# A two-layer hybrid decoder trunk: a fixed order for the opening, modulation handed out beside the first mixer's products, and linear attention in other memory

## The chip, the core and the metric

The kernel runs on one core of a Trainium2 chip. Its engines are TensorE (PE, with weight loads as PEld), VectorE (DVE), ScalarE (ACT), GpSimd (POOL) and SyncE (SP), which issues most DMAs. The metric is the device time of one execution in microseconds (us), as the median of several runs.

## What is computed

The reference is a trunk of two layers over 1024 positions of width 1024, in float32. Cut to what matters:

```python
cond = silu(c)
for l in range(2):
    sh1, sc1, gt1, sh2, sc2, gt2 = split(cond @ w_mod[l] + b_mod[l], 6)
    h = rms_norm(x, norm_g[l, 0]) * (1 + sc1) + sh1
    z = split_cols(h @ w_in[l])                  # one projection for four groups of width 256
    outs = [short_conv(z), nsa(z), gla(z), gmlp(z)]
    y = concat(rms_norm(o, grp_gain) for o in outs) @ w_o[l]
    x = x + gt1 * rms_norm(y, norm_g[l, 1])
    h = rms_norm(x, norm_g[l, 2]) * (1 + sc2) + sh2
    y = square(relu(h @ w_up[l])) @ w_down[l]    # 1024 -> 4096 -> 1024
    x = x + gt2 * rms_norm(y, norm_g[l, 3])
```

`short_conv` is a gated convolution of width 3; `nsa` is attention over compressed, selected and window keys, with rotated queries and keys; `gla` is gated linear attention in chunks; `gmlp` mixes 128 positions at a time with a triangular matrix.

## The kernel before

**Tiling.** The sequence is cut into two halves of T = 512 positions, kept transposed: a tile is 128 channels by 512 positions, and x is eight such tiles. Layer l and half hf make one `mix(l, hf)` and one `ff(l, hf)`. Products are made in float32 accuracy from rounded parts: each operand is split into a high and a low part, and `mm3` (lines 172 to 175) does three matmuls for each 128 rows of the sum. A `gemm` has eight such steps, 24 matmuls of 512 columns; its weight comes in two halves of 256 KB, each split by `wunit`, the high part by a cast on ACT (L167) and the low part by a subtraction on DVE (L131).

**Lanes.** A weight goes through the buffers of a lane: "a" and "b" with three raw buffers and four for the parts, "f" for the feed-forward part with more. Lane "b" exists during the first mixer alone; its region is released for the feed-forward lane afterwards.

**Order.** The program is written as straight code; a scheduler in the compiler orders the instructions of all engines by its own timeline, with priorities. `high_priority(offset=-LATER[l, hf])` puts the residual and the norm at the end of a mixer later (lines 950 to 956). Once compiled, each engine runs its instructions in one fixed order.

**Opening.** `start()` (L265) makes cond, loads x for half 0, makes the first norm's R (ones-product L195, ACT L199 and L200), the first two modulation vectors by dots on DVE (L239, one for every 128 outputs, two for every k) and, for each k of eight, h (L207 to L210) and one step of `mm3` for the six outputs in EARLY, so that 18 matmuls follow on each h. Their weights are w_k, in two sets of six. `rope_tables` (L339) makes cosines and sines on DVE, transposes them (L375), multiplies by a selection (L380), copies (L377, L382) and writes both to DRAM.

**First mixer.** `mix(0, 0)` runs its attention (`nsa_part`: probabilities bp are transposed into ps_t, L777, split into w_a at L779 and L131, and multiplied by values, L782 and L783) beside linear attention (`gla_part`: for each j of four a score product L592, copies, a select on POOL L596, products L602 and L605). Then come `gmlp_part` and `conv_part`, whose regions take the memory of linear attention, and then `mods_now(0, (2, 3, 4), "b")`: 48 dots on DVE (L247), each on a load of 256 KB, for the modulation that is needed behind w_o. w_o's eight gemms (L943) end in a copy to yo (L946). `norm(0, 1, xt)` of the other half stands behind them.

**End of ff(1, 0).** In the last group of `down` eight sums are added into the tiles yf (L137) of region "fin", which lies where region "wo" of `mix(1, 1)` lay. The residual (L226) and `make_h` (L203) of `mix(1, 1)` go on at that time.

## Time and profile before

| what | value |
|---|---|
| median of 3 runs | 2635.78 us (2635.64 to 2638.55) |
| profiled execution | 2634.88 us, span 2633.1 us, mean granted clock 0.975 |
| PE busy | 2488.4 us, 95% of the span |
| DVE, ACT, POOL busy | 1631.0, 1310.5, 53.0 us |
| DMA | 305.79 MB, mean 116 GB/s |

A stretch in which PE is busy for less than its length, or at a granted clock under 1, is where time can be had; who released PE at the end of an idle time is given behind the arrow in the rows.

### The profile page before, as it was taken

To read this page: it belongs to the slowest core of one execution; us is meant where nothing else is said; L and a number is where in the kernel's file an instruction comes from. 1 tells how busy PE (TensorE), PEld (TensorE's weight loads), DVE (VectorE), ACT (ScalarE), POOL (GpSimd) and SP (SyncE) were. 2 spreads that over 40 slices of the span, in tenths; PEclk is the share of its full clock that TensorE was granted. 3 is DMA by queue.
4 is the path that set the end of the run, shared out by engine and by line. 5 is a ranking of instruction groups with operands and counts; after the bars stand their busy time and mean duration, and the time that the engine had idled before them with its cause. 6 is when DMAs were issued, how large, how long until landed. Compare 5 with 4: busy or idle time off the path is not lost.

```text
span 2633.1 us, 34406 instructions
## 1 busy us (share of the span) xinstructions
PE 2488.4 (95%) x11834; PEld 1987.3 (75%) x11834; DVE 1631.0 (62%) x3425; ACT 1310.5 (50%) x2657; POOL 53.0 (2%) x65
## 2 busy tenths in 40 slices
PE   5899499999999999999999999999999998899997
PEld 3666277777877878887787878877788876788886
DVE  7676866557888577444676476544567755634445
ACT  3573345445665356344366445444466744443333
POOL 0100000000000000000100000000100000000000
PEclk9899699999999999999999999999999999999999
DMA  8313634345434454322522344322322134433332
GB/s 279 100 46 100 203 117 132 106 140 153 129 123 134 155 164 140 102 85 89 154 83 70 116 152 140 99 84 79 119 77 68 57 108 143 136 97 96 97 97 75
DMA packets 176200, 305.79 MB, mean 116 GB/s; under 512 B 21573, under 2 KB 33434, under 8 KB 176026
## 3 DMA queue, kind: packets, MB, share of 16 engines
q1 hardware_dynamic: 176026, 303.60, 36.7%
q8 instruction: 93, 1.52, 0.2%
q14 instruction: 81, 0.66, 0.1%
HBM read 281.50 MB, written 17.83 MB: 114 GB/s over the span
## 4 chain that ended last, share of the span: by engine, by line
PE 83%; DVE 6%; DMA 4%; issue 1%; ACT 1%; POOL 0%; DVEq 0%; SPq 0%; ACTq 0%; POOLq 0%
PE ps_ff L173 16%; PE ps_ff L174 16%; PE ps_ff L175 16%; PE ps_mm L173 8%; PE ps_mm L175 8%; PE ps_mm L174 8%; DMA raw_f<-in_w_mod_dram 2%; PE ps_pv L783 1%; PE ps_mm L777 1%; PE ps_pv L782 1%; PE ps_s L822 1%; DMA raw_b<-in_w_mod_dram 1%; PE ps_s L824 1%; PE ps_t L777 1%; PE ps_t L195 1%
## 5 line engine op out<-in xcount | busy, mean ns | idle before, releaser
L167 ACT CAST w_f<-raw_f 128x512 fp32r<-128x512 f32 x504 | 311.7, 619 | 426.3 <-PE ps_ff L174 409.2
L131 DVE TENSOR_TENSOR w_f<-raw_f,w_f 128x512 fp32r<-128x512 f32 x504 | 350.4, 696 | 178.7 <-ACT w_f L167 167.9
L173 PE MATMUL ps_ff<-hid,w_f 128*128 128x512 f32 x992 | 395.4, 399 | 21.7 <-DVE yf L137 12.7
L175 PE MATMUL ps_ff<-h,w_f 128*128 128x512 f32 x1024 | 405.4, 396 | 1.2 <-DVE w_f L131 1.2
L173 PE MATMUL ps_ff<-h,w_f 128*128 128x512 f32 x1024 | 403.1, 394 | 0.0
L174 PE MATMUL ps_ff<-h,w_f 128*128 128x512 f32 x1024 | 402.3, 393 | 0.0
L174 PE MATMUL ps_ff<-hid,w_f 128*128 128x512 f32 x992 | 392.4, 396 | 1.5 <-DVE hid L131 1.5
L175 PE MATMUL ps_ff<-hid,w_f 128*128 128x512 f32 x992 | 391.7, 395 | 0.0
L173 PE MATMUL ps_mm<-h,w_a 128*128 128x512 f32 x784 | 318.2, 406 | 32.6 <-ACT yo L946 23.7
L175 PE MATMUL ps_mm<-h,w_a 128*128 128x512 f32 x784 | 317.2, 405 | 6.0 <-DVE w_a L131 6.0
L174 PE MATMUL ps_mm<-h,w_a 128*128 128x512 f32 x784 | 314.8, 403 | 3.6 <-DVE h L131 3.6
L167 ACT CAST w_a<-raw_a 128x512 fp32r<-128x512 f32 x196 | 121.3, 620 | 304.5 <-PE ps_mm L174 278.7
L131 DVE TENSOR_TENSOR w_a<-raw_a,w_a 128x512 fp32r<-128x512 f32 x196 | 135.1, 689 | 179.2 <-ACT w_a L167 173.3
L173 PEld LDWEIGHTS ps_ff<-hid,w_f 128*128 128x128 f32 x992 | 188.1, 190 | 69.8 <-DVE yf L137 15.2
L175 PEld LDWEIGHTS ps_ff<-h,w_f 128*128 128x128 f32 x1024 | 192.3, 188 | 45.5 <-issue 2.9
L173 PEld LDWEIGHTS ps_ff<-h,w_f 128*128 128x128 f32 x1024 | 192.4, 188 | 43.0 <-issue 3.1
L174 PEld LDWEIGHTS ps_ff<-h,w_f 128*128 128x128 f32 x1024 | 192.4, 188 | 42.0 <-issue 2.2
L174 PEld LDWEIGHTS ps_ff<-hid,w_f 128*128 128x128 f32 x992 | 188.3, 190 | 44.6 <-issue 2.9
L175 PEld LDWEIGHTS ps_ff<-hid,w_f 128*128 128x128 f32 x992 | 187.9, 189 | 41.1 <-issue 1.4
L137 DVE TENSOR_TENSOR y<-y,ps_ff 128x512 f32<-128x512 f32 (+1 forms) x208 | 138.0, 664 | 125.0 <-PE ps_ff L175 123.8
L173 PEld LDWEIGHTS ps_mm<-h,w_a 128*128 128x128 f32 x784 | 149.9, 191 | 72.8 <-ACT yo L946 24.1
L175 PEld LDWEIGHTS ps_mm<-h,w_a 128*128 128x128 f32 x784 | 149.8, 191 | 44.5 <-DVE w_a L131 7.7
(390 smaller groups left out, 3610.2 us busy)
## 6 DMA issues: line engine op xcount, KB each, us to landing
raw_f<-in_w_up_dram SPq DMA_DIRECT2D x256, 256.0 KB, 2.7
raw_f<-in_w_down_dram SPq DMA_DIRECT2D x256, 256.0 KB, 2.7
raw_a<-in_w_in_dram SPq DMA_DIRECT2D x132, 256.0 KB, 2.6
raw_f<-in_w_mod_dram SPq DMA_DIRECT2D x112, 256.0 KB, 2.9
raw_a<-in_w_o_dram SPq DMA_DIRECT2D x64, 256.0 KB, 2.7
raw_b<-in_w_mod_dram SPq DMA_DIRECT2D x48, 256.0 KB, 3.1
mw<-in_w_mod_dram SPq DMA_DIRECT2D x16, 512.0 KB, 5.7
bp<-in_cmp_w_dram SPq DMA_DIRECT2D x32, 256.0 KB, 5.7
```

Of the source, the lines that this page charges most:

```text
L131: V.tensor_tensor(out=out, in0=a, in1=b, op=ALU.subtract)
L137: eng.tensor_tensor(out=out, in0=a, in1=b, op=ALU.add)
L167: A.copy(hi, raw)
L173: PE.matmul(ps_ap, wh, xh, start=start, stop=False)
L174: PE.matmul(ps_ap, wh, xl, start=False, stop=False)
L175: PE.matmul(ps_ap, wl, xh, start=False, stop=stop)
L195: PE.matmul(p, ones, acc, start=True, stop=True)
L777: PE.transpose(tp[0:kn, hh, :], cols(h0 + hh), ident)
L782: PE.matmul(pv[:, h0:h0 + nh, :], vst, th[0:kn], start=first[0], stop=False)
L783: PE.matmul(pv[:, h0:h0 + nh, :], vst, tl[0:kn], start=False, stop=last)
L822: PE.matmul(sp[:, 0:w], qh[:, h0 + hh, :], KX[:, 128 * k0:128 * k0 + w], start=True, stop=False)
L824: PE.matmul(sp[:, 0:w], ql[:, h0 + hh, :], KX[:, 128 * k0:128 * k0 + w], start=False, stop=True)
```

## The change

**In words.** (1) `start()` is written inside a manual schedule: its instructions keep the written order on every engine. x is loaded right behind c, parameters and rope constants by POOL's queue. The rope table is a generator: its DVE part stands at k = 0, and one piece (transposes and a copy, or a product, a copy and a write to DRAM) follows each of k = 0 to 5. h is made from x times R (DVE), an Identity with scale and bias (ACT), a cast (ACT) and a subtraction (DVE). The modulation weights are loaded three k ahead. (2) The 48 dots of `mods_now` are handed out two at a time with each weight half of lane "b" (`beside`). (3) Linear attention of the first mixer takes its tiles from the y tiles and the h tiles, so that its region need not be released before gMLP's and convolution's begin. (4) Each group's outputs are split right behind the group; attention is first, then linear attention, gMLP, convolution. (5) The first six outputs of w_o begin with the four input tiles of linear attention and attention, and are finished with the other four. (6) x of half 1 is loaded between w_o and its norm in the program. (7) At the end of ff(1, 0) the sums and the loaded x take h tiles (`spare`), and LATER of (1, 1) is 0.

```diff
-LATER = {(0, 0): 0, (0, 1): 800, (1, 0): 800, (1, 1): 800}
+LATER = {(0, 0): 0, (0, 1): 800, (1, 0): 800, (1, 1): 0}
...
         for n in names:
-            dma(out=par[l][n], in_=src[n][l])
+            P.dma_start(out=par[l][n], in_=src[n][l])
...
     def gemm(ps_ap, lane, src, h, order=(0, 1, 2, 3, 4, 5, 6, 7)):
         for kh in (order[0] // 4, order[4] // 4):
             hi, lo = wunit(lane, src[:, 4 * kh:4 * kh + 4, :], [128, 4, 128])
+            if lane in beside:
+                next(beside[lane], None)
...
+    def gemm_part(ps_ap, lane, src, h, kh, start, stop):
+        hi, lo = wunit(lane, src[:, 4 * kh:4 * kh + 4, :], [128, 4, 128])
+        for k in range(4):
+            mm3(ps_ap, hi[:, k, :], lo[:, k, :], h[4 * kh + k][0], h[4 * kh + k][1],
+                start and k == 0, stop and k == 3)
...
-        with region("kw", "right") as kw, region("su") as su:
+        with region("kw", "right") as kw, region("rp") as rp, region("su") as su, tc.manual_schedule():
...
+            xt = load_x(0)
+            tables = rope_tables(rp)
             for hf in range(2):
...
                 logsig(t2, ch, t1)
                 A.activation(t2, t2, AF.Exp)
                 mul(ch, ch, t2)
-            xt = load_x(0)
-            load_params(0, ("ng", "bmod"))
+            ms = [mload(0)]
+            raws = wload(0)
+            ms += [mload(1), mload(2)]
             R = rms_R(xt, 1.0 / 1024)
...
             for k in range(8):
...
+                msum(k, ms[k])
+                if k == 0:
+                    next(tables)
+                if k < 5:
+                    ms.append(mload(k + 3))
+                if k == 2:
+                    raws = wload(1)
+                mul(xt[k], xt[k], R)
                 if k % 4 == 0:
-                    raws = [wload(n, k // 4) for n in EARLY]
-                hs += make_h(xt, R, d["A1"], d["mod"][:, 0, :], (k,))
-                if k % 4 == 0:
-                    ws = {n: wsplit(r) for n, r in zip(EARLY, raws)}
+                    wsplit(raws)
+                t = nt()
+                A.activation(t, xt[k], AF.Identity, scale=d["A1"][:, k:k + 1], bias=d["mod"][:, 0, k:k + 1])
+                hs.append(split(t))
                 for i, n in enumerate(EARLY):
...
+                next(tables, None)
...
             for hf in range(2):
+                yield
                 tp = ps("t", (17, 4, 128))
...
                 for w, dst in ((0, cosd), (128, sind)):
-                    p = ps("s")
+                    yield
+                    p = ps("pv")
...
-                    dma(out=dst[hf], in_=o)
+                    P.dma_start(out=dst[hf], in_=o)
...
         def gt(shape=(128, T)):
+            if opening:
+                return work.tile(list(shape), F32, name="g", tag="y", bufs=8)
             return rg.tile(list(shape), F32, name="g", tag="g", bufs=10)
...
-        qx = gt((128, 4, 128))
-        sb = gt((128, 2, 2, 128))
-        am = gt((128, 4, 128))
+        qx = ht((128, 4, 128))
+        sb = ht((128, 2, 2, 128))
+        am = ht((128, 4, 128))
...
-                with region("wb", "right") as lane_pool["b"]:
-                    with region("gl", "right") as rg:
-                        gates, lrT = gate_part(l, hf, h, gr, rg, "a", early)
-                        yn = nsa_part(l, hf, h, es.enter_context(region("ns")), gates, early)
-                        ol = gla_part(l, hf, h, rg, "b", sx, lrT)
-                    with region("cv", "right") as rg, region("gm", "right") as rg2:
-                        og = gmlp_part(l, hf, h, rg2, "b", sx)
-                        oc = conv_part(l, hf, h, rg, "b", sx)
-                    mods_now(0, (2, 3, 4), "b")
+                with region("wb", "right") as lane_pool["b"], region("gl", "right") as rg, \
+                        region("cv", "right") as rgc, region("gm", "right") as rgm:
+                    beside["b"] = mods_now(0, (2, 4, 3), "b")
+                    gates, lrT = gate_part(l, hf, h, gr, rg, "a", early)
+                    yn = nsa_part(l, hf, h, es.enter_context(region("ns")), gates, early)
+                    on = [split(t) for t in group_out(yn, "t", gain[:, 2:4])]
+                    ol = [split(t) for t in gla_part(l, hf, h, rg, "b", sx, lrT)]
+                    og = [split(t) for t in gmlp_part(l, hf, h, rgm, "b", sx)]
+                    oc = [split(t) for t in conv_part(l, hf, h, rgc, "b", sx)]
+                    for _ in beside.pop("b"):
+                        pass
...
+            if opening:
+                for o in range(6):
+                    sums[o] = ps(("mm", "mm", "ff", "ff", "s", "s")[o])
+                    gemm_part(sums[o], "a", w_o[l, o], outs, 1, True, False)
             for o in range(8):
+                if o in sums:
+                    p = sums[o]
+                    gemm_part(p, "a", w_o[l, o], outs, 0, False, True)
+                else:
+                    p = ps("mm")
+                    gemm(p, "a", w_o[l, o], outs, range(8))
...
         with region("fin") as rg:
-            down(NGRP - 1, yo=lambda: rg.tile([128, T], F32, name="yf", tag="yf", bufs=8))
+            down(NGRP - 1, yo=(lambda: rg.tile([128, T], F32, name="yf", tag="yf", bufs=8)) if l == 0 else spare)
...
-    xt = load_x(1)
-    h = mix(0, 0, h, lambda: norm(0, 1, xt), early)
+    h = mix(0, 0, h, lambda: norm(0, 1, load_x(1)), early)
```

**ACT in the opening.** Before, from R on (line 200) to the second set of w_k; h at L209 is the high part, written directly:

```order
L200 ACTIVATE nt_281<-nt_281 128x512
L209 ACTIVATE h_307<-nt_305,mod0_100 128x512
L209 ACTIVATE h_370<-nt_368,mod0_100 128x512
L209 ACTIVATE h_403<-nt_401,mod0_100 128x512
L209 ACTIVATE h_436<-nt_434,mod0_100 128x512
L209 ACTIVATE h_481<-nt_479,mod0_100 128x512
```

After, from the end of the first set of w_k (L291); L337 is the Identity of one k, L232 the cast of h, L413 and L419 copies of the rope pieces from ps_t and ps_pv:

```order
L291 CAST w_k_301<-raw_k_195 128x512
L291 CAST w_k_305<-raw_k_197 128x512
L337 ACTIVATE nt_309<-y_151,mod0_100,A10_101 128x512
L232 CAST h_311<-nt_309 128x512
L413 COPY nt_344<-ps_t_339 17x512
L337 ACTIVATE nt_356<-y_153,mod0_100,A10_101 128x512
L232 CAST h_358<-nt_356 128x512
L419 COPY of_382<-ps_pv_380 128x512
L337 ACTIVATE nt_407<-y_155,mod0_100,A10_101 128x512
L232 CAST h_409<-nt_407 128x512
L419 COPY of_433<-ps_pv_431 128x512
```

The h of each k stood alone on ACT behind the other; now a copy of a rope piece, which reads what PE makes behind the 18 matmuls of k, stands between the cast of k and the Identity of k+1.

**PE at the end of the first mixer's attention.** Before, steps of attention (L777, L782, L783) and of linear attention (L592, L602, L605) in turn:

```order
L782 MATMUL ps_pv<-w_a,VW 128x512
L783 MATMUL ps_pv<-w_a,VW 128x512
L777 MATMUL ps_t<-ident,bp 128x128 x4
L602 MATMUL ps_ff<-g 64x128 x2
L605 MATMUL ps_ff<-g 128x64 x2
L602 MATMUL ps_ff<-g 64x128 x2
L605 MATMUL ps_ff<-g 128x64 x2
L592 MATMUL ps_ff<-g 128x512
L782 MATMUL ps_pv<-w_a,VW 128x512
L783 MATMUL ps_pv<-w_a,VW 128x512
L777 MATMUL ps_t<-ident,bp 128x128 x4
L602 MATMUL ps_ff<-g 64x128 x2
```

After, the same operations are L821, L826, L827 and L636, L646, L649; L205 is the ones-product of attention's norm:

```order
L821 MATMUL ps_t<-ident,bp 128x128 x4
L826 MATMUL ps_pv<-w_a,VW 128x512
L827 MATMUL ps_pv<-w_a,VW 128x512
L821 MATMUL ps_t<-ident,p 32x128 x4
L826 MATMUL ps_pv<-w_a,VC 128x512
L827 MATMUL ps_pv<-w_a,VC 128x512
L205 MATMUL ps_t<-nt,ones 128x512
L636 MATMUL ps_ff<-gh,g 128x512
L646 MATMUL ps_ff<-gh,g 64x128 x2
L649 MATMUL ps_ff<-g,gh 128x64 x2
L646 MATMUL ps_ff<-gh,g 64x128 x2
L649 MATMUL ps_ff<-g,gh 128x64 x2
```

The steps of attention now all stand ahead of that norm, and linear attention's all behind it, with no lane-b matmul among them.

**DVE at the end of ff(1, 0).** Before, from the ninth of make_h's sixteen steps on (every row but one has two); yo, A_112 and mod_109 belong to make_h of `mix(1, 1)`, yf to the sums of `ff(1, 0)`:

```order
L140 SCALAR_TENSOR_TENSOR nt<-yo,A_112,nt 128x512 x2
L140 SCALAR_TENSOR_TENSOR h<-nt,mod_109,h 128x512 x2
L140 SCALAR_TENSOR_TENSOR nt<-yo,A_112,nt 128x512 x2
L137 TENSOR_TENSOR yf<-y,ps_ff 128x512 x2
L140 SCALAR_TENSOR_TENSOR h<-nt,mod_109,h 128x512 x2
```

After, from the same step on; the sums are the tiles sp:

```order
L140 SCALAR_TENSOR_TENSOR nt<-yo,A_112,nt 128x512 x2
L140 SCALAR_TENSOR_TENSOR h<-nt,mod_109,h 128x512 x2
L140 SCALAR_TENSOR_TENSOR nt<-yo,A_112,nt 128x512 x2
L140 SCALAR_TENSOR_TENSOR h<-nt,mod_109,h 128x512 x2
L137 TENSOR_TENSOR sp<-y,ps_ff 128x512 x2
L137 TENSOR_TENSOR nt<-nt 128x512
```

The first two additions into the sums stood behind fourteen of make_h's sixteen steps, and stand now behind all sixteen.

## Rows read from the trace of the kernel before

**Rows 1.** stages: us, busy PE, PEld, DVE, ACT, POOL (x), clock, DMA, GB/s
```profile
0.00:40.00 40.00, 11.57 (x19) 3.70 (x19) 26.14 (x72) 17.92 (x32) 1.51 (x9) 1.00 0.88 299
40.00:75.00 35.00, 34.99 (x144) 28.13 (x144) 27.21 (x59) 10.43 (x17) 1.18 (x1) 1.00 0.74 249
75.00:102.50 27.50, 17.00 (x191) 14.81 (x190) 19.23 (x58) 13.09 (x45) 7.26 (x6) 0.69 0.29 77
102.50:256.00 153.50, 149.04 (x782) 114.02 (x781) 104.45 (x274) 90.83 (x222) 4.85 (x8) 0.98 0.22 66
256.00:319.30 63.30, 19.74 (x56) 12.29 (x55) 56.94 (x153) 23.17 (x39) 0.64 (x1) 0.63 0.64 203
319.30:350.00 30.70, 30.70 (x122) 24.67 (x123) 11.30 (x20) 11.95 (x21) 0.00 (x0) 0.92 0.43 135
```

**Rows 2.** PE's waits: tile and line, releaser: us in total, times, longest
```profile
PE ps_mm L173 <- ACT yo L946: 23.7, 1, 23.7
PE ps_ff L173 <- DVE yf L137: 12.7, 3, 12.1
PE ps_mm L173 <- ACT h L222: 7.0, 1, 7.0
```

**Rows 3.** timeline of PE, opening: start, us, row, idle before and releaser
```profile
16.97 3.78 PE L380 MATMUL ps_s<-nt,sl 17*128 17x512 f32 x4 [1.81 <-ACT nt L377]
26.36 2.04 PE L195 MATMUL ps_t<-nt,ones 128*128 128x512 f32 x2 [5.61 <-DVE nt L137]
40.00 1.22 PE L173 MATMUL ps_mm<-h,w_k 128*128 128x512 f32 x2 [11.59 <-ACT h L209]
```

**Rows 4.** ACT by lines, 0 to 75: busy us, mean ns, idle before
```profile
L282 ACT CAST w_k<-raw_k 128x512 fp32r<-128x512 f32 x12 | 6.8, 616 | 4.7 <-DMA raw_k<-in_w_in_dram 2.9 <-PE ps_mm L174 1.8
L209 ACT ACTIVATE h<-nt,mod 128x512 fp32r<-128x512 f32 x8 | 5.8, 723 | 24.2 <-DVE nt L140 24.2
L382 ACT COPY of<-ps_s 128x512 f32<-128x512 f32 x4 | 2.3, 573 | 0.0
```

**Rows 5.** DVE by lines, 0 to 75 us
```profile
L239 DVE CUSTOM_DVE_ANT_0 mw<-mw,cond 128x1024 f32<-128x1024 f32 x16 | 19.3, 1220 | 1.0 <-DMA mw<-in_w_mod_dram 0.9
L131 DVE TENSOR_TENSOR w_k<-raw_k,w_k 128x512 fp32r<-128x512 f32 x12 | 7.8, 686 | 5.9 <-ACT w_k L282 5.9
L140 DVE SCALAR_TENSOR_TENSOR sn<-sn,x 128x64 f32<-128x64 f32 x5 | 1.1, 219 | 0.0
```

**Rows 6.** a short wait of PE and the four us behind it
```profile
370.52 0.50 PE L175 MATMUL ps_mm<-h,w_a 128*128 128x512 f32 x1 [2.61 <-DVE w_a L131]
...
370.50:374.50 4.00, 3.98 (x12) 3.19 (x13) 4.00 (x7) 1.28 (x3) 0.00 (x0) 0.69 0.97 347
```

**Rows 7.** DVE's modulation dots, by lines, 256 to 319.3 us
```profile
L247 DVE CUSTOM_DVE_ANT_0 raw_b<-raw_b,cond 128x512 f32<-128x512 f32 x43 | 29.4, 687 | 6.3 <-DMA raw_b<-in_w_mod_dram 6.2
```

**Rows 8.** casts of attention's end (ACT), selects of linear attention (POOL)
```profile
194.17 0.57 ACT L779 CAST w_a<-ps_t 128x512 fp32r<-128x512 f32 x1
196.89 0.59 ACT L779 CAST w_a<-ps_t 128x512 fp32r<-128x512 f32 x1 [1.08 <-PE ps_t L777]
...
182.47 0.68 POOL L596 TENSOR_SCALAR_AFFINE_SELECT g<-g 128x512 f32<-128x512 f32 x1 [3.92 <-ACT g L595]
187.06 0.64 POOL L596 TENSOR_SCALAR_AFFINE_SELECT g<-g 128x512 f32<-128x512 f32 x1 [3.92 <-PE ps_t L777]
```

**Rows 9.** the end of ff(1,0): PE, DVE and the window
```profile
2230.92 2.08 PE L195 MATMUL ps_t<-nt,ones 128*128 128x512 f32 x2 [5.15 <-DVE nt L137]
2245.08 0.79 PE L173 MATMUL ps_ff<-hid,w_f 128*128 128x512 f32 x1 [12.08 <-DVE yf L137]
...
2234.42 1.41 DVE L140 SCALAR_TENSOR_TENSOR nt<-yo,A,nt 128x512 f32<-128x512 f32 x2 [3.55 <-ACT nt L200]
...
2244.35 1.28 DVE L137 TENSOR_TENSOR yf<-y,ps_ff 128x512 f32<-128x512 f32 x2
...
2229.00:2249.00 20.00, 6.00 (x11) 3.64 (x12) 14.51 (x22) 8.68 (x13) 0.00 (x0) 0.50 0.54 186
```

## What the change does to the time: a prediction

> **What bounds the kernel now.** I read the busy time by stages first [rows 1]. TensorE (PE) is the bound: from 102.5 to 256 us it is busy for 149.0 of 153.5 us. It stands still at the beginning, at 75 to 102.5, and at 256 to 319.3, where it is busy for 19.7 of 63.3 us at a granted clock of 0.63. After 350 us nearly everything is PE's work. The list of PE's waits [rows 2] says what ended the idle time: 23.7 us behind a copy of w_o's sum on ScalarE (ACT), 12.7 us behind additions into the tile yf, 7.0 behind make_h; the first two are single long waits. So the change can win at three places: before the first product (at 40.00 us [rows 3]), between 256 and 319.3, and at the end of ff(1,0). I go through them in the order of time, and everything is compared with the profiled execution: 2634.9 us, a span of 2633.1 and 1.8 around it. The median of the runs is 0.9 higher.
>
> **The opening: x first, order by hand.** Before, the ones-product of the first norm starts at 26.36 and the first product at 40.00 [rows 3]. After, x is loaded directly behind c. ACT has eight steps for c and eight squares ahead of the sum, 16 x 0.62 us [rows 4] = 10 us from the arrival of c. The small loads for the rope table had arrived about 4.5 us before PE's first row at 8.75, since the table has some 20 dependent VectorE (DVE) steps of 0.22 us [rows 5]; c arrives a little later, I take 6.5. So the sum of squares is there at 16.5. Then DVE does in its written order two modulation dots (2 x 1.22), the rope table (4.5), x times R (0.7), six low halves of w_k and one of h (7 x 0.69) [rows 5]: 12.4 us, so the first full product can run at about 29, which is 11 us earlier than before.
>
> This gain is spent at once. Before, all rope products were done by 20.7, and PE ran its 144 matmuls from 40 to 75 without a gap [rows 1]. After, a piece of the rope table (transposes or a product, on PE behind the 18 matmuls of k) follows each of k = 0 to 5, and on ACT its copy stands ahead of the Identity of k+1. ACT works in its order: the copy waits until PE has finished k, and only then can the next h be made: copy 0.57, Identity 0.72, cast 0.62 (the mean of ACT's cast, [rows 4]), the low half on DVE 0.69 [rows 5], 2.6 us in which PE has nothing. Behind k = 3 six casts of the second w_k stand there too (6 x 0.53 at their pitch, 3.2 us, estimated from the 0.62 each takes). So: 29.2 for the first full product, 35.0 for the 144 matmuls as before [rows 1], 5.8 for the rope pieces that now lie on the path (3.8 for four products of 0.95 [rows 3] and two groups of transposes at 1.0), 6 x 2.6 = 15.6, 3.2: 88.8.
>
> The clock comes on top. At 370.52 a gap of 2.61 us was followed by 4.0 us at a granted clock of 0.69 [rows 6], so about 1.24 us were lost. The six gaps of the opening are as long and 5 us apart: 6 x 1.24 = 7.4, and the opening ends at 96 in place of 75, +21 us. Bounds: no loss of clock, gaps of 2 us and a first product at 27 give +8; a slow clock for all of every k's 18 matmuls (4.1 us at full clock, 8.2 at half) and 30 for the start give +27. The Trainium skill, page "TensorE: Matmul & The Clock Gate", section "HAM oscillation — how this bites in real kernels", tells of a kernel whose groups of matmuls are set apart by idle waits and which starts every group slow anew; by that rule every k here would begin slow, and without it the opening would end at 89 and the whole be 7 us shorter. The trace agrees at the one gap of [rows 6].
>
> **75 to 102.5.** This stretch is a chain of rotations, gates and compressions in which PE is busy for 17.0 and DVE for 19.2 of 27.5 us [rows 1]. Lane b's first loads now hand out modulation, eight dots of 0.69 [rows 7] in DVE's queue ahead of the first lane-b product: 5.5 us at most, nothing at least; since DVE is the busier engine there I take +4.
>
> **102.5 to 350, the modulation moved, and linear attention in other memory.** What goes is large. Between 256 and 319.3 PE lost 43.6 us idle and 19.7 x 0.37 = 7.3 us of clock [rows 1]: 51 us. The 48 dots there (43 in the window with 29.4 us of DVE, [rows 7]) ran alone; they now lie beside lane b's 32 half products, two to a half for the first 24, and w_o's first six outputs begin with the half that needs only attention and linear attention. The 23.7 us wait [rows 2] goes, nothing as long follows it, as PE then has w_o's sums in turn.
>
> What comes, from the order of after: 18 of the 32 halves (216 matmuls) stand ahead of the attention's last steps; then come twelve groups of transposes with their products and no lane-b matmul, then linear attention's four steps, then gMLP, conv and w_o. (a) The 18 halves: PE's busy time in the stage is 149.0; 384 lane-b matmuls at 0.227 (222 fill 50 us in the later dense stretches) are 87 of it, so 62 are other work, some 23 of that in (b) and 3 in gMLP. That leaves 49 + 36 = 85 us for PE. DVE's 104.5 us [rows 1], less what follows later (about 44: lane-b low halves of 14 products, gMLP, conv, linear attention and the last attention steps), plus some 30 further dots of 0.69, is 81. Two engines with nearly equal loads in a fixed order do not fit perfectly: 90. (b) A step of the attention's end is transposes into the one ps_t buffer, a cast on ACT, a low half on DVE, a product: the casts follow each other at 2.72 us [rows 8], at 1.9 if only busy times counted (0.66 + 0.58 + 0.69). Twelve at 2.5: 30. The norm of that group, 7.5 (two additions, a square, a sum, the ones-product, two ACT steps, two scalings, two low halves). Linear attention: the selects on GpSimd (POOL), one for each j, are 4.59 us apart [rows 8]; before, attention's steps lay in these gaps, now nothing does: 4 x 4.57 = 18.3. Its norm 7, and about 4.5 in which PE waits for the third lane-b weight, since that weight's low half is queued on DVE behind gMLP's normalisation. 67 in all, of which PE works 23. (c) The remaining 168 lane-b and 192 w_o matmuls are 360 x 0.227 = 81.7, with gMLP's and the norms' products and small gaps 90. Sum 247, against 247.5 before. The 51 us are won and given back: about 5 in (a), 44 in (b), the rest in (c). Bounds: 224 (busy times alone) to 262 (lane b slower by 0.5 us a half, steps at 2.72, a slow clock behind each).
>
> Since x(1) is loaded later but long before its norm, and the parameters go by POOL's queue, I count nothing for both; PE's order behind w_o is as before.
>
> **The end of ff(1,0).** PE waits 5.15 us for a norm's sum and 12.08 for yf, the clock is at 0.50 and PE busy for 6.0 of the 20 us at 2229 to 2249 [rows 9]: 17 us with the clock. The change gives these sums other tiles and (1,1) another priority. But the wait is DVE's order: the first additions into yf stand behind fourteen of the sixteen steps of make_h, which start at 2234.42 when R comes [rows 9], and in the order of after they stand behind all sixteen. So the 17 us stay: 0 (two more steps of 0.75 would add 1.4).
>
> **Sum.** 2634.9 + 21 + 4 + 0 + 0 = 2659.9; with the median's 0.9, 2661.
>
> **Rivals.** First, the middle runs at busy times: hand-overs between the engines hide behind each other, (a) takes 85, the attention's steps 1.9 each, the wait for the third weight is gone. That is 5 + 7 + 4.5 and some 6 in norms and small gaps, 23 us less: 2638, not slower. It decides if the stretch from the first lane-b product to w_o's end takes less than 228 us. For it speaks that DVE's busy share between 102.5 and 256 is 0.68 and PE's 0.97; against it, that the casts are 2.72 apart although ACT and DVE are free between them [rows 8].
>
> Second, the bubble at 2229 does go, because the sums wait for memory and not for the queue: 17 us less, 2644. For it speaks that yf's tiles lie where w_o's outputs lay; against it DVE's order.
>
> Third, more is lost: lane b's three raw buffers now carry weights and modulation in turn, and a load waits for the dot that frees its buffer behind all that is queued on DVE. 43 dots took 63.3 us alone, 1.47 us each; a half with three loads that way takes 4.4 us at least, and with a wait of 1.1 behind attention's steps 5.5, so (a) takes 99; and every k of the opening is slow throughout, +5. 2661 + 9 + 5 = 2675.
>
> **How the numbers follow.** Forecast 0.48, first rival 0.22, second 0.08, third 0.22. Within 0.2%, about what a measurement of this kernel can tell from no change, is 2630.5 to 2641. Slower by more: 0.43 of the forecast, 0.06 of the first, 0.02 of the second, all of the third, 0.73. Within: 0.03 + 0.08 + 0.03 = 0.14. Faster: 0.02 + 0.08 + 0.03 = 0.13. The range goes from the first rival with an opening at its lower bound (2638 - 13 = 2625) to the third with the middle at its upper bound, 2692.
>
> **What would show it.** The opening: between the k's of the first products gaps of 2 to 3 us that end with h, a granted clock under 0.9 from 30 to 95, and the last of the 144 matmuls at 90 to 100; wrong, if they run without gaps. The middle: a stretch of 55 to 70 us in which PE is busy by a third, with ACT's casts and POOL's selects one after the other; wrong, if matmuls with w_b lie in it. The 63 us of modulation alone must be gone; if PE again waits over 10 us for yo, that step is wrong. The end of ff(1,0): a wait of 10 to 13 us for DVE's sum must still be there. The forecast falls as a whole if the first lane-b product starts before 110 us.

## The result: slower by 1.7%

The changed kernel takes 2681.5 us in the median of four runs (2674.2 to 2685.6), the kernel before 2635.71 us beside it. The ratio is 1.017, with a 95% interval of 1.0145 to 1.0195: 45.8 us are lost where 25 were forecast. The profiled execution took 2680.05 us with a span of 2678.3, against 2634.88 and 2633.1, so 45.2 us are to be found in the two traces.

The windows of the kernel after, cut at the same points of the program as in [rows 1] where there are such points, and the last one at the end of ff(1,0):

```profile
0.00:28.30 28.30, 2.11 (x3) 0.54 (x3) 19.32 (x58) 16.77 (x27) 8.02 (x20) 1.00 0.90 321
28.30:100.60 72.30, 54.15 (x160) 37.14 (x160) 35.71 (x73) 18.33 (x30) 3.44 (x5) 0.86 0.40 131
100.60:131.50 30.90, 17.57 (x187) 15.27 (x187) 25.09 (x74) 12.90 (x43) 8.29 (x7) 0.58 0.47 136
131.50:210.00 78.50, 77.07 (x419) 61.09 (x418) 66.05 (x219) 50.46 (x133) 0.00 (x0) 0.97 0.54 164
210.00:307.40 97.40, 59.15 (x170) 30.93 (x168) 41.94 (x114) 34.27 (x77) 4.62 (x8) 0.54 0.17 56
307.40:400.00 92.60, 91.17 (x406) 72.27 (x405) 60.07 (x101) 44.98 (x79) 0.00 (x0) 0.98 0.32 103
2274.00:2294.00 20.00, 5.70 (x12) 3.41 (x13) 13.56 (x20) 8.08 (x12) 0.00 (x0) 0.52 0.06 21
```

The last of the 144 matmuls on w_k ends at 100.6 in place of 75.0, and the first product of lane b starts at 131.5 in place of 102.5. The eight sums of w_o are copied to yo by this row of line 1002, whose last copy was at 355.7 before:

```profile
L1002 ACT COPY yo<-ps_mm x4: 577/578/578, 373.2 to 399.2; 128x512 f32<-128x512 f32 x4
```

So the account is +25.6 in the opening, +3.4 between it and lane b, +14.5 from lane b's first product to the last yo (267.7 in place of 253.2), 43.5 us up to there, and 1.0 at the end of ff(1,0). The remaining 0.7 is spread over the rest.

The middle is worth one more look, since its loss is of another kind than idle time. This is that stretch in both traces, the kernel before first:

```profile
102.50:355.70 253.20, 205.18 (x983) 155.53 (x983) 174.76 (x448) 128.42 (x285) 5.49 (x9) 0.89 0.35 110
```
```profile
131.50:399.20 267.70, 226.59 (x987) 163.62 (x986) 167.39 (x432) 128.95 (x287) 4.62 (x8) 0.82 0.33 104
```

PE's rows are the same work. Its idle time fell from 48.0 to 41.1 us, so the change did what it says, a little. But its busy time rose by 21.4 us, at a granted clock of 0.82 in place of 0.89.

PE's waits after: tile and line, releaser, us in total, times, longest. They answer to [rows 2]:

```profile
PE ps_t L205 <- DVE nt L137: 26.9, 4, 17.6
PE ps_mm L175 <- ACT h L232: 23.9, 7, 8.6
PE ps_ff L175 <- DVE sp L137: 13.6, 1, 13.6
PE ps_mm L754 <- DMA p<-in_cmp_pos_dram: 5.8, 1, 5.8
```

The 23.7 us behind yo are gone. Of the seven waits for h in the opening the first, 8.6 us, stands ahead of the first product; the other six, five of 2.03 or 2.04 us and one of 5.15 behind k = 3, are new. The wait for yf has become one for sp, of 13.6 in place of 12.1 us.

The opening on PE and on ACT (start, us, row, idle time before and releaser), against [rows 3]:

```profile
17.62 2.08 PE L205 MATMUL ps_t<-nt,ones 128*128 128x512 f32 x2 [17.62 <-DVE nt L137]
28.27 0.79 PE L175 MATMUL ps_mm<-h,w_k 128*128 128x512 f32 x1 [8.57 <-ACT h L232]
30.98 0.79 PE L176 MATMUL ps_mm<-h,w_k 128*128 128x512 f32 x1 [1.92 <-DVE h L131]
40.44 0.73 PE L175 MATMUL ps_mm<-h,w_k 128*128 128x512 f32 x1 [2.03 <-ACT h L232]
49.70 0.49 PE L175 MATMUL ps_mm<-h,w_k 128*128 128x512 f32 x1 [2.04 <-ACT h L232]
```
```profile
38.44 0.57 ACT L413 COPY nt<-ps_t 17x512 f32<-17x512 f32 x1 [10.23 <-PE ps_t L411]
38.92 0.81 ACT L337 ACTIVATE nt<-y,mod,A 128x512 f32<-128x512 f32 x1
39.76 0.62 ACT L232 CAST h<-nt 128x512 fp32r<-128x512 f32 x1
47.70 0.59 ACT L419 COPY of<-ps_pv 128x512 f32<-128x512 f32 x1 [7.32 <-PE ps_pv L417]
```

The order of waits can be read off the two fences. ACT is idle for 10.23 us until PE has made the transposes behind k = 0, copies them, and only then makes the next h (Identity at 38.92, cast at 39.76); PE has by then waited 2.03 us.

In the middle, selects of linear attention on POOL and casts of attention's end on ACT, against [rows 8]:

```profile
266.61 0.64 POOL L640 TENSOR_SCALAR_AFFINE_SELECT gh<-gh 128x512 f32<-128x512 f32 x1 [8.61 <-ACT gh L639]
273.49 0.63 POOL L640 TENSOR_SCALAR_AFFINE_SELECT gh<-gh 128x512 f32<-128x512 f32 x1 [6.25 <-ACT gh L639]
```
```profile
240.90 0.58 ACT L823 CAST w_a<-ps_t 128x512 fp32r<-128x512 f32 x1 [2.46 <-PE ps_t L821]
243.95 0.58 ACT L823 CAST w_a<-ps_t 128x512 fp32r<-128x512 f32 x1 [2.46 <-PE ps_t L821]
```

The steps are one behind the other, as forecast, but longer: 6.88 us from select to select, where 4.59 had been measured, and 3.05 from cast to cast, where 2.72 had been.

The end of ff(1,0), PE and DVE, against [rows 9]:

```profile
2274.68 2.08 PE L205 MATMUL ps_t<-nt,ones 128*128 128x512 f32 x2 [4.61 <-DVE nt L137]
2290.38 0.80 PE L175 MATMUL ps_ff<-hid,w_f 128*128 128x512 f32 x1 [13.62 <-DVE sp L137]
```
```profile
2278.18 1.41 DVE L140 SCALAR_TENSOR_TENSOR nt<-yo,A,nt 128x512 f32<-128x512 f32 x2 [3.55 <-ACT nt L210]
...
2289.65 1.28 DVE L137 TENSOR_TENSOR sp<-y,ps_ff 128x512 f32<-128x512 f32 x2
```

From 2278.18 to 2289.65 DVE does the sixteen steps of make_h and nothing else, and then the additions that PE waits for.

### The profile page after: what moved, and what is told of

It reads as the page before. It is cut to its first block, busy times and chain, and to the rows that moved or that the text cites. A ratio compares the mean times of both kernels' runs of the same rounds, so it can differ in the third digit from the quotient of the medians.

```text
span 2678.3 us, 34430 instructions
## 1 busy us (share of the span) xinstructions
PE 2519.2 (94%) x11834; PEld 1998.0 (75%) x11834; DVE 1630.3 (61%) x3425; ACT 1317.4 (49%) x2665; POOL 62.2 (2%) x80
## 4 chain that ended last, share of the span: by engine, by line
PE 82%; DVE 8%; DMA 6%; ACT 2%; issue 2%; POOL 0%; SPq 0%; DVEq 0%; POOLq 0%; ACTq 0%
PE ps_ff L175 16%; PE ps_ff L176 16%; PE ps_ff L177 16%; PE ps_mm L176 7%; PE ps_mm L177 7%; PE ps_mm L175 7%; DMA raw_f<-in_w_mod_dram 3%; PE ps_pv L827 1%; DMA raw_b<-in_w_mod_dram 1%; PE ps_pv L826 1%; PE ps_mm L821 1%; PE ps_t L205 1%; PE ps_s L866 1%; PE ps_t L821 1%; PE ps_s L868 1%
## 5 line engine op out<-in xcount | busy, mean ns | idle before, releaser
L175 PE MATMUL ps_ff<-hid,w_f 128*128 128x512 f32 x992 | 395.4, 399 | 23.3 <-DVE sp L137 13.6
L177 PE MATMUL ps_mm<-h,w_a 128*128 128x512 f32 x752 | 301.9, 402 | 5.5 <-DVE w_a L131 5.5
L175 PE MATMUL ps_mm<-h,w_a 128*128 128x512 f32 x752 | 302.9, 403 | 2.5 <-ACT w_a L167 1.7
L176 PE MATMUL ps_mm<-h,w_a 128*128 128x512 f32 x752 | 299.1, 399 | 0.0
L177 PEld LDWEIGHTS ps_mm<-h,w_a 128*128 128x128 f32 x752 | 142.1, 189 | 42.2 <-DVE w_a L131 7.4
L175 PEld LDWEIGHTS ps_mm<-h,w_a 128*128 128x128 f32 x752 | 142.1, 189 | 39.4 <-issue 3.6
```

The costliest lines, as they stand in the source:

```text
L175: PE.matmul(ps_ap, wh, xh, start=start, stop=False)
L176: PE.matmul(ps_ap, wh, xl, start=False, stop=False)
L177: PE.matmul(ps_ap, wl, xh, start=False, stop=stop)
```

## Experiments

Each ratio is to the kernel before on the same chip, with its 95% interval; the changed kernel stands at 1.017. A difference in us to the changed kernel is the difference of the ratios times 2635.7; it carries the interval of the changed kernel, about 7 us either way, beside its own.

### The middle: attention's norm behind linear attention

One line moved:

```diff
-                    on = [split(t) for t in group_out(yn, "t", gain[:, 2:4])]
                     ol = [split(t) for t in gla_part(l, hf, h, rg, "b", sx, lrT)]
+                    on = [split(t) for t in group_out(yn, "t", gain[:, 2:4])]
```

> The changed kernel with one line moved: attention's group output and its split stand behind linear attention in the program instead of ahead of it, so that linear attention's three h tiles come ahead of attention's four in the ring of h tiles. Theory B (the place of these tiles in the ring, and with it DVE's order, kept linear attention's four steps behind all of attention): the four steps lie again between attention's last steps, the stretch from 210 to 307 us shrinks by the 27 us of the steps and some 8 of the norm, 2640 to 2650. Rival (attention's last steps at half clock bound the stretch anyway, linear attention only takes their time): 2665 to 2680.

Measured: 2628.77 us, ratio 1.0000 (0.9989 to 1.0011), 45 us less than the changed kernel and more than was expected. The last copy to yo is at 351.2 in place of 399.2, though the first lane-b product still starts at 131.4. The windows from 225 to 250 us, the changed kernel first:

```profile
225.00:250.00 25.00, 18.52 (x48) 10.43 (x48) 7.69 (x15) 4.95 (x9) 0.00 (x0) 0.50 0.06 21
```
```profile
225.00:250.00 25.00, 21.88 (x94) 12.60 (x92) 13.22 (x37) 13.18 (x36) 1.91 (x3) 0.80 0.24 77
```

In the same 25 us 94 rows of PE are done in place of 48, since steps of linear attention lie among those of attention again, and products with w_b follow from 255.7 in place of 307.4. The place of one group's norm in the program was what kept the two groups apart.

### The middle: is it the memory or the order?

Linear attention's tiles now come from the ring of h tiles, and so do the split outputs of attention's norm, so that the moved line also changes which of them takes its buffers first. Here the tiles alone are taken ahead, and the order stays:

```diff
+    early_gh = []
...
-            return hp.tile(list(shape), F32, name="gh", tag="h", bufs=32) if opening else gt(shape)
+            return early_gh.pop(0) if opening else gt(shape)
...
                     yn = nsa_part(l, hf, h, es.enter_context(region("ns")), gates, early)
+                    for shape in ((128, 4, 128), (128, 2, 2, 128), (128, 4, 128)):
+                        early_gh.append(hp.tile(list(shape), F32, name="gh", tag="h", bufs=32))
```

> The changed kernel with the three h tiles of linear attention taken from the ring ahead of attention's four, while attention's output stays ahead of linear attention in the program. Moving attention's output behind linear attention had won 45 us, and that edit changed both the place in the ring and the program's order. Theory B (the ring): the same gain, ratio 1.000 to 1.003. Theory I (the program's order, by which the scheduler places attention's end and its norm ahead of linear attention on DVE and PE): nothing changes, ratio 1.015 to 1.019.

Measured: 2673.46 us, ratio 1.0170 (1.0153 to 1.0187). It is the changed kernel's time, and the selects are 6.88 us apart as there. The theory of the ring, which was also put forward for the moved line, falls; what decides is the program's order.

### The middle: what makes a step of linear attention 6.88 us long

Each score product is made a second time, into a tile that nothing reads:

```diff
             PE.matmul(att, k1[:, 128 * j:128 * j + 128], qx, start=True, stop=True)
+            if opening:
+                PE.matmul(ps("s", (128, 4, 128)), k1[:, 128 * j:128 * j + 128], qx, start=True, stop=True)
```

> The changed kernel (ratio 1.017) with one more score product of 512 columns on PE behind each of linear attention's four, its result read by nothing; it lies where PE waits 1.65 us for POOL's select. Theory G' (linear attention's step takes 6.88 us instead of the 4.57 before because PE's own products in it run at half clock): with PE busy through the wait the clock rises to full within the four steps, the steps go to 4.5 to 5.5 us, 4 to 9 us are won, ratio 1.0135 to 1.0155. Rival (the step is as long as its hand-overs whatever the clock): the extra product of 2.0 us at half clock exceeds the wait, 1 to 3 us more, ratio 1.0175 to 1.018.

Measured: 2672.25 us, ratio 1.0135 (1.0120 to 1.0150), about 9 us less with more work in it; its interval and the changed kernel's just touch, and the trace is plainer. The selects, and the window from 250 to 275 us (the changed kernel has a clock of 0.50 there):

```profile
271.55 0.64 POOL L642 TENSOR_SCALAR_AFFINE_SELECT gh<-gh 128x512 f32<-128x512 f32 x1 [4.46 <-PE ps_s L638]
276.12 0.65 POOL L642 TENSOR_SCALAR_AFFINE_SELECT gh<-gh 128x512 f32<-128x512 f32 x1 [3.92 <-PE ps_s L638]
280.68 0.63 POOL L642 TENSOR_SCALAR_AFFINE_SELECT gh<-gh 128x512 f32<-128x512 f32 x1 [3.92 <-ACT gh L641]
```
```profile
250.00:275.00 25.00, 14.29 (x47) 6.52 (x48) 11.76 (x34) 8.36 (x19) 1.91 (x3) 0.63 0.13 38
```

At a granted clock of 0.63, and 0.78 in the 25 us behind it, the steps are 4.57 us apart, what they were in [rows 8]. PE's small products in a step (out of the tiles gh and g into ps_ff) are 0.44 and 0.66 us long here, 0.69 and 1.12 in the changed kernel. The chain of hand-overs had not become longer; PE in it had become slower.

### The middle: modulation behind convolution again

The dots go back behind the groups, while the memory of linear attention stays as changed:

```diff
-                    beside["b"] = mods_now(0, (2, 4, 3), "b")
+                    mods = mods_now(0, (2, 4, 3), "b")
...
-                    for _ in beside.pop("b"):
+                    for _ in mods:
                         pass
```

> The changed kernel with the 48 modulation dots written behind convolution again, instead of two with each half of lane b's weights; the memory stays that of the changed kernel. Theory E (the pacing itself won the 51 us of modulation that stood alone): the dots stand alone again behind convolution, less some 14 us that w_o's first halves cover, so 2710 to 2720. Rival F (the memory that lets the regions stand beside each other is enough, since the scheduler then moves the dots forward into DVE's idle time at the end of attention): 2672 to 2686.

Measured: 2688.8 us, ratio 1.0227 (1.0210 to 1.0244), 15 us more than the changed kernel and between the theories. The wait for yo is back:

```profile
PE ps_mm L175 <- ACT yo L1002: 20.6, 1, 20.6
```

But the net is 15, not 21: here the 144 matmuls end at 97.1 and the first lane-b product starts at 122.2, 25.1 us later, where the changed kernel needs 30.9. Its wait of 5.8 us for the load of in_cmp_pos is not in this trace. So handing out modulation costs 6 us between the opening and lane b; behind lane b's first product it takes 18 us off (285.5 us up to the last yo here, 267.7 in the changed kernel).

Another 3.5 us lie in the opening, which is written as in the changed kernel (97.1 against 100.6, at a clock of 0.90 against 0.86). ACT's first copies of rope pieces show what they are:

```profile
38.39 0.57 ACT L413 COPY nt<-ps_t 17x512 f32<-17x512 f32 x1 [9.61 <-PE ps_t L411]
46.35 0.58 ACT L419 COPY of<-ps_pv 128x512 f32<-128x512 f32 x1 [6.01 <-PE ps_pv L417]
55.92 0.58 ACT L419 COPY of<-ps_pv 128x512 f32<-128x512 f32 x1 [7.62 <-PE ps_pv L417]
```

From the first to the second are 7.96 us, where the changed kernel has 9.26, and from the second to the third 9.57 in both. PE's gap ahead of k = 1, 2, 3, 5 and 6 is 2.03 or 2.04 us in both traces; k = 1, 3 and 5 ran at the full clock here, k = 2, 4 and 6 had a slow stretch. So such a gap did not always bring a slow stretch, and the opening moves with it: in six traces of kernels with this opening it ends between 97.1 and 100.7.

### The opening: all pieces of the rope table last

```diff
                     mm3(early[n], hi[:, k % 4, :], lo[:, k % 4, :], hs[k][0], hs[k][1], k == 0, k == 7)
-                next(tables, None)
+            for _ in tables:
+                pass
```

> The changed kernel (2681.5 us) with the six rope pieces behind the eighth k instead of one behind each of k = 0 to 5; nothing else is changed. Theory A (ACT's copy of a rope piece, which waits for the end of k's matmuls on PE, is what sets the k apart): the 144 matmuls run without gaps of 2 us and end near 68 us instead of 100.5; the table is then made later, which gives back up to 10 us before the first lane-b product, so 2650 to 2658. Rival (the modulation dots, their loads or the making of h on DVE set the pace of the opening): the k stay 8 to 9 us apart, and the time stays within 6 us of 2681.

Measured: 2667.43 us, ratio 1.0143 (1.0128 to 1.0159), 7 us less than the changed kernel, far less of a gain than theory A said and just outside the rival's 6 us. The last of the 144 matmuls ends at 76.4, 24 us earlier, but lane b starts only here:

```profile
121.35 0.77 PE L175 MATMUL ps_mm<-h,w_b 128*128 128x512 f32 x1
```

That is 45 us behind the 144 matmuls in place of 31: rotations need the table, which is late now. The first rotation on POOL starts at 91.76 here, 15 us behind the matmuls, after a wait of 4.3 us for a load of the table; in the changed kernel it starts at 99.35, ahead of their end. So theory A had the cause right, since the k are 5.5 us apart here, and the price of the late table too low. The pieces took 24 us of the opening, where the forecast's terms for them (5.8, 15.6 and 7.4) make 28.8, and the table is needed soon after it. Having them early is right; having them in the way of h is not.

### The opening: h one step ahead

The pieces stay, but h of k + 1 is written ahead of k's products and piece:

```diff
-            for k in range(8):
+            def prep(k):
...
+            for k in range(8):
+                if k == 0:
+                    prep(0)
+                if k % 4 == 0:
+                    wsplit(raws)
+                if k < 7:
+                    prep(k + 1)
```

> The changed kernel (ratio 1.017 to before) with h of k+1 written ahead of the products and the rope piece of k, so that on ACT the Identity and the cast of k+1 no longer stand behind a copy that waits for PE; the rope pieces stay one behind each k. The last run of this kind (rope pieces all behind the eighth k) ended the 144 matmuls at 76 us instead of 100.5, but the first lane-b product came only 10 us earlier. Theory A (ACT's order sets the k apart, and there the late table took 14 us back): the 144 matmuls end at 76 to 82 and the first lane-b product comes at 107 to 113 instead of 131.5, so 18 to 24 us are won, ratio 1.008 to 1.010. Rival (the 31 us behind the opening are a chain that needs ACT and DVE for itself and grows when the opening shrinks): 7 us as before, ratio 1.014.

Measured: 2655.8 us, ratio 1.0097 (1.0082 to 1.0112), 19 us less. ACT's timeline around the first piece:

```profile
36.36 0.81 ACT L336 ACTIVATE nt<-y,mod,A 128x512 f32<-128x512 f32 x1 [4.53 <-DVE y L134]
37.20 0.62 ACT L232 CAST h<-nt 128x512 fp32r<-128x512 f32 x1
37.73 0.57 ACT L420 COPY nt<-ps_t 17x512 f32<-17x512 f32 x1
```

The copy now stands behind the next h. The 144 matmuls end at 80.5 and lane b starts at 112.8 in place of 131.5: the serial order was worth all of these 19 us, 20 in the opening. What stays is PE's wait for the casts of w_k, 10.3 us, of which 9.1 lie ahead of the first product.

### The opening: how much of it is the clock

Seven matmuls into a tile that nothing reads follow each piece, so that PE is busy while ACT makes h:

```diff
                 next(tables, None)
+                if k < 6:
+                    warm = ps("pv" if k % 3 == 0 else "t")
+                    for _ in range(7):
+                        PE.matmul(warm, hs[k][0][:, 0:128], hs[k][0], start=True, stop=True)
```

> The changed kernel with seven more matmuls of 512 columns on PE behind the rope piece of each of k = 0 to 5, whose results nothing reads; the order of all else is kept, and ACT's wait with it. Theory G (about 2 us of each k's 9.4 us is the slow clock that each short wait brings): PE has no idle time left between the k, the clock holds at 1.0, each k takes 7.2 to 7.8 us, 10 to 13 us are won, ratio 1.012 to 1.013. Rival H (the clock is not set by these waits; the fillers only add their own time, 7 x 0.43 less the 2.0 of the wait): 0 to 6 us more, ratio 1.017 to 1.019.

Measured: 2670.49 us, ratio 1.0152 (1.0137 to 1.0167), 5 us less, under what was expected and within the intervals. The trace is plainer. The copies behind the pieces of k = 1 and 2:

```profile
45.82 0.59 ACT L423 COPY of<-ps_pv 128x512 f32<-128x512 f32 x1 [6.03 <-PE ps_pv L421]
53.80 0.59 ACT L423 COPY of<-ps_pv 128x512 f32<-128x512 f32 x1 [6.03 <-PE ps_pv L421]
```

k = 1, 2, 3 and 5 take 7.4 to 8.0 us here and 9.0 to 9.6 in the changed kernel, at a clock of 0.97 and of 0.86 in the opening. So in that execution the clock took 1.3 to 1.6 us of each of these k, 6 in the opening, whose end is at 94.2 in place of 100.6 (and of 97.1 at the least in the six traces with the opening as it was). The 2 us of each gap itself are the order's.

### The end of ff(1,0): sums in place

The last group's sums for layer 1 are added into y itself, with no tile of their own:

```diff
-            down(NGRP - 1, yo=(lambda: rg.tile([128, T], F32, name="yf", tag="yf", bufs=8)) if l == 0 else spare)
+            down(NGRP - 1, yo=(lambda: rg.tile([128, T], F32, name="yf", tag="yf", bufs=8)) if l == 0 else None)
```

> The changed kernel with the last sums of ff(1, 0) added into the y tiles in which they already stand, instead of into h tiles. Theory C (the additions waited because their new tiles, first in a region and now in the ring of h tiles, came free or were given out only behind make_h, and this put them behind make_h in DVE's order): the waits of 4.6 and 13.6 us at 2270 to 2290 go down to under 5 together, 2664 to 2670. Rival D (nothing is won: ff(1, 1) then waits for the y tiles, or R's chain holds PE whatever the order): 2676 to 2684.

Measured: 2657.64 us, ratio 1.0108 (1.0091 to 1.0124), 16 us less. The window around the place:

```profile
2240.00:2290.00 50.00, 46.62 (x197) 36.36 (x196) 40.07 (x63) 27.49 (x46) 0.00 (x0) 1.00 0.42 141
```

PE is busy for 46.62 of 50 us at full clock; its longest wait for a sum in it is 1.71 us. The same edit in the kernel before:

```diff
-            down(NGRP - 1, yo=lambda: rg.tile([128, T], F32, name="yf", tag="yf", bufs=8))
+            down(NGRP - 1, yo=(lambda: rg.tile([128, T], F32, name="yf", tag="yf", bufs=8)) if l == 0 else None)
```

> The kernel before with the last sums of ff(1, 0) added in place into the y tiles, nothing else changed. Theory C (new tiles for these sums put their additions behind make_h on DVE, before as after): the waits of 5.15 and 12.08 us of [rows 9] and their slow clock go, 14 to 17 us, ratio 0.9935 to 0.9945. Rival D (in the kernel before the region that held the sums was not what they waited for): 0.999 to 1.001.

Measured: 2620.41 us, ratio 0.9942 (0.9925 to 0.9958), 15 us less than before. The bubble of [rows 9] stands in both kernels, and the same edit takes it away in both.

### The three edits together, and pacing in them

The edits of "attention's norm behind", "h one step ahead" and "sums in place" in one kernel, and then the same with the dots behind convolution:

```diff
-                    beside["b"] = mods_now(0, (2, 4, 3), "b")
+                    mods = mods_now(0, (2, 4, 3), "b")
```

> The changed kernel with three edits together: h of k+1 ahead of the products of k, attention's output behind linear attention, the last sums of ff(1, 0) in place. If the three losses lie one behind the other and are independent, their gains add: 18 to 24, 45 and 16 us off a ratio of 1.017, so 0.984 to 0.987, some 37 us under the kernel before. Rival (the gains overlap: a faster opening only moves the wait to the loads or to DVE between 130 and 210 us, where DVE is busy for 23 of 25 us): 0.990 to 0.994.

> The three edits of the best kernel so far (ratio 0.983), with the modulation dots written behind convolution again instead of two with each half of lane b's weights. In the changed kernel this cost 15 us (ratio 1.0227 against 1.017): the dots went to the end of the first mixer, where w_o's sums waited 20.6 us for copies behind make_h, but the stretch of lane b's products was faster. Theory E: pacing is worth 10 to 20 us here too, ratio 0.987 to 0.991. Rival (with attention's end and linear attention side by side DVE has no room beside lane b, and the dots are better off behind): 0.979 to 0.983.

Measured: 2586.7 us, ratio 0.9832 (0.9817 to 0.9847), for the three together, faster than both kernels. Singly they were worth 45, 19 and 16 us, 80 in all, together 89, no more apart than the intervals. Its stretch from lane b's first product to the last yo:

```profile
112.80:328.50 215.70, 205.26 (x979) 154.79 (x979) 165.39 (x429) 125.73 (x283) 6.55 (x8) 0.95 0.40 129
```

215.7 us in place of 267.7, with 10.4 us idle at a clock of 0.95. With the dots behind convolution it is 2603.51 us, ratio 0.9876 (0.9862 to 0.9891), and PE waits for yo again:

```profile
PE ps_mm L175 <- ACT yo L1009: 16.3, 1, 16.3
```

So pacing is worth 0.44% here, some 12 us, and 15 in the changed kernel: this idea of the change holds with either order around it.

## Why the prediction was right, and where it was too small

**The opening: +21 forecast, +25.6 measured; right in mechanism.** The first norm's ones-product was to start 10 us earlier, behind squares at 16.5; it started at 17.62. The first full product was put at 29.2 and came at 30.98. That gain was to be spent by ACT's order, a rope copy ahead of each h. The trace shows these rows one by one, and the h-ahead run gave 20 us of the opening back. Five gaps are 2.03 or 2.04 us as PE sees them, under the 2.6 assumed, but a slow stretch took 1.3 to 1.6 us of a k where 1.24 was taken from the single gap of [rows 6]; and behind k = 3 the six casts of w_k came as said, 3.21 us of ACT's time at 66.74, with a gap of 5.15 us.

The forecast cited the Trainium skill, page "TensorE: Matmul & The Clock Gate", section "HAM oscillation — how this bites in real kernels", for groups of matmuls that are set apart by waits and each start slow, and took it that every k would. The waits told of there are waits for loads, longer than these gaps, so the page does not decide this case, and the trace agrees in part. These are matmuls of k = 1 in the changed kernel, two near its beginning and two near its end:

```profile
42.18 0.63 PE L175 MATMUL ps_mm<-h,w_k 128*128 128x512 f32 x1
42.60 0.63 PE L176 MATMUL ps_mm<-h,w_k 128*128 128x512 f32 x1
...
45.54 0.39 PE L177 MATMUL ps_s<-h,w_k 128*128 128x512 f32 x1
45.77 0.39 PE L175 MATMUL ps_s<-h,w_k 128*128 128x512 f32 x1
```

They are 0.42 us apart behind the gap and 0.23 later: k = 1 starts at the low level of the clock, and so does k = 4. But k = 2, 3, 5 and 6 start at the high level and fall within 2 us of their first matmul, and in the run with the dots behind convolution three k stay at the high level throughout. So "every k slow from its start" is more than the traces show; that most of these gaps cost a slow stretch is shown. The end without a loss of clock was put at 89; with the fillers, where k = 4 still starts slow, it was 94.2.

**75 to 102.5: +4 forecast, +3.4 measured; the place was right, the path only in part.** The cost was put on dots in DVE's queue ahead of the first lane-b product. Seven dots lie there, and without pacing the stretch is 6 us shorter (25.1 us; with the three edits 25.2 against 32.3). But PE's longest wait in it is 5.8 us for the load of in_cmp_pos, against 3.4 in the kernel before, and that load was issued late: SP issued it at 116.47, and ahead of it in SP's queue stood a load into raw_b that had waited 4.2 us, up to 114.82, for a dot on DVE (L257) to free its buffer. This is the third rival's mechanism, at another place. In other runs with paced loads the same wait of PE, 5.5 to 5.8 us, ends with low or high parts of the queries on DVE, so which of the two paths costs how much is not separated. That +4 came out near +3.4 is in part chance: no term of it stood for the load.

**The middle: 0 forecast, +14.5 measured; the failed term is (b).** (a) took 78.5 us where 90 was said, near the 85 of the busy times; the two nearly equal loads did fit. (c) took 92.6 where 90 was said. (b), the attention's last steps, linear attention and the norms with PE a third busy, was put at 67 and took 97.4. By its own terms: attention's steps up to 251.9 took 41.9 in place of 30 (twelve lay there, as said, but the first four took 4.4 us each, with exponentials of the last scores on ACT among them up to 223.6, and the others 3.05 to 3.6 where 2.5 was said), the norm to 263.6 took 11.7 in place of 7.5, linear attention 27.5 in place of 18.3, and the last norm with gMLP's beginning 16.3 in place of 11.5. All four were priced with rows from a stage in which the granted clock was 0.98 [rows 1, 8], while the forecast itself had PE a third busy, and the neighbouring stretch with PE at a third, 256 to 319.3, stood in [rows 1] at 0.63. The clock in (b) was 0.54. The extra score product showed the price for linear attention: 4.57 us a step at the better clock. For the attention's steps the run with the moved line has them at a granted clock of 1.00, between 246 and 251 us:

```profile
248.18 0.60 PE L821 MATMUL ps_t<-ident,bp 128*128 128x128 f32 x4
250.53 0.60 PE L821 MATMUL ps_t<-ident,bp 128*128 128x128 f32 x4
```

There 2.35 to 2.67 us lie from one group of transposes to the next, and PE's wait for the cast is 0.68 us as in the changed kernel, whose transposes are 1.05 us long and whose step is 3.05. So 0.4 to 0.7 us of a step are the clock, by estimate 4 to 8 of the 12 us by which these steps were put too short, and the 2.5 assumed holds at full clock only.

The mechanism of (b) held: no matmul with w_b lies between 210 and 307.4, and the moved line showed that the program's order of two groups made it so. Its sign did not come as said, a stretch of 55 to 70 us with PE busy by a third: it was 97.4 us with PE busy for 59.2, since the same products take longer at the low clock. The 4.5 us put on a lane-b weight appeared as 4.55 us behind an ACT copy for gMLP instead.

A second slip lies in the comparison itself: the forecast's 247 us end with w_o, but were set against a stage that ends at 350, while w_o's last copy before is at 355.7, 253.2 us behind lane b's first product. By that mark the three terms promised a gain of 6, and against it they missed by 21: 11.5 too much in (a), 30.4 too little in (b), 2.6 too little in (c), less 0.8 from the last copy to 400. That (a) was too dear is luck for the forecast: without it the whole would have been short by 32 us and not by 20.5.

**The modulation alone.** The forecast said that the stretch of 63 us and the yo wait go and that nothing so long follows. That is so: no wait for yo over 10 us remains, and 41 dots now lie between 131.5 and 400.

**The end of ff(1,0): 0 to 1.4 forecast, +1.0 measured.** DVE's order was the reason given, and the rows at 2278.18 to 2289.65 show all sixteen steps ahead of the sums. The rival that it would go with the new memory falls: the sums got other tiles and waited still. That they need no tile at all was not thought of; without one the wait is gone, and 15 to 16 us with it, in both kernels. So it was the tiles of their own that put the sums behind make_h in DVE's order; by which step of the scheduler is not shown.

**The rivals.** The middle at busy times, 2638, was right for (a) alone. The third rival comes nearest in number, 2675, but falls in (a), where it had loads wait for dots: (a) was faster than the forecast, not slower. Its 26 us for the opening are near the 25.6 measured, yet no k was slow throughout. The upper end of the range does not come out of its terms, since 2675 and 15 for the middle are 2690 and not 2692; nothing hangs on it here. The conditions under which the whole forecast would have fallen did not come: the first lane-b product was at 131.5, not ahead of 110.

**What stays open.** Why one gap of 2.03 us brings a slow stretch and another does not; and why the fillers' gain of 6.4 us at the end of the opening is 4.6 us at the first lane-b product. Of the 30.4 us by which (b) was put too short, linear attention's 9.2 are shown to be the clock and 4 to 8 in attention's steps are an estimate; the 9.0 of the two norms were not tried. The parts (3), (5) and (6) of the change were not taken out singly, so what each is worth is not shown.

## What to carry to other kernels

When work is run beside other work, look in the program's order for the last thing of one group that stands ahead of the first thing of the next: one norm written between two chains was worth 45 us, and one copy ahead of the next h 19 us. Price a chain in which PE is a third busy with rows from a stretch with such a share, at the clock granted there, not with the same operations' rows from a full stretch. A number that comes out right by another path than the one it was given for is not yet understood; take the step out and measure it.

## What was not expected of the hardware

Adding work made a stretch shorter, twice: a second score product, with a result that nothing reads, took a step of linear attention from 6.88 to 4.57 us and the kernel from a ratio of 1.017 to 1.0135, and seven such matmuls for each of six k took four of them from 9.0 to 9.6 us down to 7.4 to 8.0 (for the whole kernel that difference is within the intervals). Once PE fell to the low level in a chain in which it is one of the links, the chain itself became longer, and PE stayed there: the granted clock was 0.50 through 50 us, from 225 to 275, with PE busy for 18.52 and 11.65 of 25 us. And the same opening does not always bring it about: behind equal gaps of 2.03 us its k = 1 took 9.26 us in one trace and 7.96 in another.
